# Gate rows by broadcast DMA, a transpose moved one step earlier, and three groups of instructions dealt later

## The chip, the cores and the metric

The kernel runs on one core of a Trainium2 chip. Its engines run side by side, each with its own instruction order: PE (TensorE, matrix products and transposes), DVE (VectorE), ACT (ScalarE), POOL (GpSimd), and SP, which here only issues DMA transfers. The metric is the device time of one execution in microseconds.

## What is computed

Two transformer-like blocks on x [1024, 1024] in fp32. The lines that matter:

```python
# first block
h = rms_norm(x, pre_mix_g) * (1.0 + sc1) + sh1         # sh1, sc1, g1, ...: silu(c) @ w_ada + b_ada
proj = h @ w_in                                        # qk_ml, v_ml, o_ml, gates, q_at, kv_at
h_ml = mlstm_chunkwise(q_ml, k_ml, v_ml, i_pre, logf)  # 4 heads of 128
h_ml = rms_norm(h_ml, ml_norm_g) * sigmoid(o_ml)
o_at = rms_norm(sliding_window_attention(q_at, k_at, v_at, attn_sinks), attn_norm_g)  # 8 heads of 64, window 128
x = x + g1 * rms_norm(concatenate([h_ml, o_at]) @ w_out, post_mix_g)
x = x + g2 * rms_norm(conv_ffn(rms_norm(x, pre_ffn_g) * (1.0 + sc2) + sh2), post_ffn_g)   # width 2816
# second block
x = x + concatenate([attention(h), pool_mixer(h)]) @ w_out_2          # h = rmsnorm(x, norm1_g_2) @ w_in_2
h = rmsnorm(x, norm2_g_2)
x = x + (silu(h @ w_gate_2) * (h @ w_up_2)) @ w_down_2                # width 2816
```

## The kernel before

The 1024 rows are eight tiles of 128 (`NT`). Every large fp32 product is made of three products of a split operand: `split` (lines 107 to 118) writes a high part (on ACT, POOL or DVE, lines 113 to 117) and, on DVE, the rest (line 118); `mm3` issues the three matmuls (lines 123 to 125). `sums_turn` transposes a tile of h (line 1313), scales it on ACT into `rawB` (lines 1297, 1299) and, for tiles 4 to 7, makes sums and differences of tiles on DVE (line 1317); `sums_split` and `part_of` split them. `one`, `two`, `three` and `five` are the products of an FFN that makes seven products of half-blocks instead of eight; `prep_first`, `prep_b1` and `prep_b2` load and split its weights. `sums_tile` is `sums_turn` and, for the first four tiles, `sums_split`.

SBUF tiles come from pools of few slots (U has 17, W 11, R 3), and PSUM from the banks that `psum(d, m, f)` sets out: in the first mixer two tiles D of two banks (`Dps`), two M (`Mps`) and two F (`Fps`); at an FFN's start two M and six F. A tile waits for the last reader of the slot that it takes. The order in which the functions are called is the program's order. A planner then deals the instructions to the engines: each engine runs its instructions in the dealt order, chosen by the planner's own costs and, among instructions that are ready by these costs, by program order. All DMAs go through SP's queue, in its order; a transfer that waits for data holds those behind it.

The stages that the change touches, in order of time:

- The opening, `start`: it loads the tiles of x (line 350), makes the shift `shp` in PSUM, copies it to SBUF as `sh` on ACT (line 362), and then normalises tile by tile (`norm`, lines 367 to 375), tile 0 with `shp` (line 372) and the others with `sh` (line 374); `to_hT` transposes (line 174).
- The sliding-window attention in `mixer1`: a loop over 16 jobs (tile n, head group g) with `turn`, `scores`, `q_stage` and, three steps behind (`LAG`), `values`. Behind a tile's second group, `values` squares the tile on ACT (line 527), sums the squares over the partitions by four products with a column of ones into an F bank (line 530, eight PE instructions as the trace counts them), copies the sum to `rat` (line 531), scales the tile on POOL (line 532) and stores it in `oad` (line 533). Behind the loop `rat` is turned into a factor, and a loop over eight groups of the q/k product (`m`) follows.
- `gates` leaves in `A` one row of 128 numbers for each of 32 pairs of chunk and head.
- The mLSTM loop at the end of `mixer1`: steps t = 0 to 10. A step does `ml_prep(t-3)` (transposes of a chunk's h, line 644, and its split `ho`, lines 647 and 648), `ml_front(t)`, `ml_mid(t-1)`, `at_part(t-2)`, for some t `tr(t-4)` (`sums_turn` of a finished tile), and `ml_part(t-3)` (the product of `ho` with its addition at line 659, post-norm, residual, store to `x1d` at line 663, pre-norm). `ml_front` loads `v` and `ogd` of a chunk into `vo` (lines 832, 833), spreads the gate rows of its four heads over the partitions by four products of 32 rows (line 836) into an M bank, adds, masks (line 838), exponentiates (839), multiplies by the k·q products (842, 843), and transposes k (850). `ml_mid` uses the result W a step later (line 882).
- The end of that loop and the start of the first FFN (lines 693 to 725).
- The second FFN's entry: a loop over tiles n (lines 1251 to 1268) that loads x3, adds the output product in two halves of 512 columns (line 1259), stores x4 (1262), normalises (POOL, 1265), and calls `sums_tile(n-1)` between the two halves; behind it `one(0)`, `sums_tile(7)`, `one(1)` to `one(3)`.

The loop of the second FFN's entry in short:

```python
for half in range(2):
    ...                                                   # 12 matmuls into ps
    nc.vector.tensor_tensor(xr[:, hs], xr[:, hs], ps, op=ALU.add)      # L1259
    if n and not half:
        self.sums_tile(h4.pop(n - 1), n - 1)
nc.sync.dma_start(out=self.x4d[n * P:(n + 1) * P, :], in_=xr)          # L1262
```

## Time and profile before

| | us |
|---|---|
| median of 3 executions (lowest to highest) | 2372.38 (2372.25 to 2374.23) |
| the profiled execution | 2373.33 |
| span of the profiled execution | 2371.5 |
| PE busy | 2275.5 (96%) |
| DVE busy | 1548.6 (65%) |
| ACT busy | 936.0 (39%) |
| POOL busy | 483.1 (20%) |
| mean granted clock of PE | 0.988 of full speed |

The page gives the busy time of each engine over the whole span. Its chain of work that ended last, followed back from the end, is almost all PE. The trace can then be asked for a stretch: busy time by engine, the waits of an engine by line with what released it ("PE f L123 <- ACT ho L647" is a wait of PE at line 123, for tile f, released by ACT's writing of `ho` at line 647), and the instructions in order of time. Times count from the span's start. The name of a tile (f, m and d are PSUM banks) stands before the line; PEld is PE's weight load, beside its matmuls.

### The profile page before, as it was taken

How to read it: one execution, taken by the hardware profiler on the slowest of the kernel's cores; microseconds unless marked ns; L12 is line 12 of the kernel's file. 1: busy time of each engine (PE TensorE's matmuls, PEld its weight loads, DVE VectorE, ACT ScalarE, POOL GpSimd, SP SyncE). 2: the span in 40 equal slices, each digit the busy share in tenths (PEclk: the TensorE clock that was granted, in tenths of full speed). 3: DMA queues.
4: the chain of work that ended last, by engine and by line, in shares of the span. 5: the costliest groups of instructions: out<-in, count | busy, mean ns of one | idle time of the engine just before them, and what ended most of it. 6: DMA issues, size and time to landing. Idle time of an engine off the chain costs nothing. (4 is left out here: it accounts for less than half of the span.)

```text
span 2371.5 us, 28426 instructions
## 1 busy us (share of the span) xinstructions
PE 2275.5 (96%) x10735; PEld 1855.0 (78%) x10735; DVE 1548.6 (65%) x2058; ACT 936.0 (39%) x1712; POOL 483.1 (20%) x570
## 2 busy tenths in 40 slices
PE   6999999998999999999989898999899999999999
PEld 3878888886787888888877786887678888888887
DVE  6757667568987777766566447995675555556661
ACT  3356424565544444511133227995542222231110
POOL 3146422232000100000021236763200000000000
PEclk9999999999999999999999999999999999999999
DMA  8612325421232222453122320001332222245301
GB/s 300 209 35 76 117 64 160 156 83 64 99 110 77 80 87 80 158 186 112 63 90 82 100 96 16 21 1 63 117 114 80 80 80 80 80 168 213 95 31 71
DMA packets 75619, 236.85 MB, mean 100 GB/s; under 512 B 11213, under 2 KB 16077, under 8 KB 75482
## 3 DMA queue, kind: packets, MB, share of 16 engines
q1 hardware_dynamic: 75482, 235.04, 29.4%
q8 instruction: 84, 1.38, 0.2%
q14 instruction: 53, 0.43, 0.1%
HBM read 184.66 MB, written 50.35 MB: 99 GB/s over the span
## 5 line engine op out<-in xcount | busy, mean ns | idle before, releaser
L123 PE MATMUL f<-h,sh 128*128 128x512 f32 x1232 | 482.8, 396 | 7.0 <-DVE d L1431 2.6
L124 PE MATMUL f<-h,sh 128*128 128x512 f32 x1232 | 485.4, 394 | 2.2 <-DVE h L118 2.2
L125 PE MATMUL f<-h,sl 128*128 128x512 f32 x1056 | 416.4, 395 | 0.1
L123 PEld LDWEIGHTS f<-h,sh 128*128 128x128 f32 x1232 | 232.0, 188 | 66.9 <-ACT d L1448 5.6
L1015 DVE TENSOR_TENSOR y<-y,f 128x512 f32<-128x512 f32 x240 | 161.2, 683 | 176.0 <-PE f L125 175.7
L124 PEld LDWEIGHTS f<-h,sh 128*128 128x128 f32 x1232 | 231.8, 188 | 55.9 <-DVE h L118 3.1
L125 PE MATMUL f<-h,h 128*128 128x512 f32 x704 | 274.1, 389 | 0.5 <-DVE h L118 0.5
L123 PE MATMUL f<-h,h 128*128 128x512 f32 x704 | 274.3, 390 | 0.0
L124 PE MATMUL f<-h,h 128*128 128x512 f32 x704 | 273.9, 389 | 0.0
L125 PEld LDWEIGHTS f<-h,sl 128*128 128x128 f32 x1056 | 198.6, 188 | 46.8 <-DVE sl L118 1.0
L117 POOL TENSOR_SCALAR sh<-raw 128x1024 fp32r<-128x1024 f32 x36 | 47.9, 1330 | 681.9 <-DVE sl L118 501.9
L125 PEld LDWEIGHTS f<-h,h 128*128 128x128 f32 x704 | 132.1, 188 | 28.3 <-DVE h L118 0.9
L124 PEld LDWEIGHTS f<-h,h 128*128 128x128 f32 x704 | 132.2, 188 | 27.5
L123 PEld LDWEIGHTS f<-h,h 128*128 128x128 f32 x704 | 132.2, 188 | 27.3
L123 PE MATMUL f<-hi,h 128*128 128x512 f32 (+2 forms) x384 | 141.0, 367 | 1.2 <-ACT qr L470 0.9
L125 PE MATMUL f<-hi,h 128*128 128x512 f32 (+2 forms) x384 | 138.2, 360 | 2.2 <-DVE h L178 2.2
L124 PE MATMUL f<-lo,h 128*128 128x512 f32 (+2 forms) x384 | 138.4, 360 | 0.0
L118 DVE TENSOR_TENSOR sl<-raw,sh 128x1024 fp32r<-128x1024 f32 x88 | 112.2, 1275 | 15.8 <-ACT sh L113 11.4
L117 POOL TENSOR_SCALAR h<-raw 128x1024 fp32r<-128x1024 f32 x26 | 32.2, 1239 | 411.0 <-PE f L125 164.4
L1452 DVE TENSOR_TENSOR d<-d,f 128x512 f32<-128x512 f32 x44 | 30.2, 686 | 118.9 <-PE f L125 118.9
L113 ACT ACTIVATE h<-raw 128x1024 fp32r<-128x1024 f32 x26 | 27.4, 1056 | 186.4 <-PE f L125 117.6
L113 ACT ACTIVATE sh<-raw 128x512 fp32r<-128x512 f32 (+1 forms) x96 | 80.1, 862 | 33.5 <-DVE raw L1403 30.5
(329 smaller groups left out, 4595.2 us busy)
## 6 DMA issues: line engine op xcount, KB each, us to landing
ada<-w_ada SPq DMA_DIRECT2D x48, 512.0 KB, 5.1
raw<-w_up SPq DMA_DIRECT2D x48, 512.0 KB, 4.2
raw<-w_gu SPq DMA_DIRECT2D x48, 512.0 KB, 3.8
raw<-w_down SPq DMA_DIRECT2D x44, 512.0 KB, 4.1
hr<-hidd SPq DMA_DIRECT2D x44, 512.0 KB, 5.5
hidd<-z SPq DMA_DIRECT2D x22, 512.0 KB, 2.6
hidd<-d SPq DMA_DIRECT2D x22, 512.0 KB, 2.7
raw<-w_out SPq DMA_DIRECT2D x16, 512.0 KB, 4.9
```

The source lines that it names most:

```text
L113: nc.scalar.activation(hi, src, AF.Copy)
L117: nc.gpsimd.tensor_scalar(hi, src, 1.0, 0.0, op0=ALU.mult, op1=ALU.add)
L118: (lo_eng or nc.vector).tensor_tensor(lo, src, hi.bitcast(F32), op=ALU.subtract)
L123: nc.tensor.matmul(out, a[0], b[0], start=start, stop=False, skip_group_check=more)
L124: nc.tensor.matmul(out, a[0], b[1], start=False, stop=False, skip_group_check=more)
L125: nc.tensor.matmul(out, a[1], b[0], start=False, stop=stop, skip_group_check=more)
L1015: nc.vector.tensor_tensor(y[:, hs], y[:, hs], ps, op=ALU.add)
L1452: nc.vector.tensor_tensor(d[:, 512:1024], d[:, 512:1024], c, op=ALU.add)
```

## The change

- In `start`, ACT's copy of `sh` comes between `norm(0)` and `norm(1)` instead of ahead of the loads of x.
- In `values`, the square stays; the sum of squares by PE, the copy to `rat`, POOL's product and the store go into `values_end`, which is called one step later ahead of the next `values`. The last one, and the factor `rat`, move into the q/k loop at m = 1.
- `gates` stores its 32 rows `A` to DRAM (`gated`), and `ml_front` loads a chunk's four rows, spread to 128 partitions (256 KB), into the upper half of `w1` by DMA, in place of the four products into an M bank.
- At the end of the mLSTM loop `ml_prep(7)` comes a step sooner, behind the new `psum`; `ml_part(6)` goes ahead of `sums_split(0)` and `tr(4)`; `tr(5)` and `sums_split(2)` go behind `ml_part(7)`.
- In the second FFN's entry `sums_tile(n-1)` follows both halves of tile n, and `one(1)` goes ahead of `sums_tile(7)`.

```diff
--- before.py
+++ after.py
@@ -309,6 +309,7 @@
         self.modr = self.dp.tile([6, D], F32, name="modr")
         self.vmd = self.dp.tile([NT, P, 512], F32, name="vmd")
         self.ogd = self.dp.tile([NT, P, 512], F32, name="ogd")
+        self.gated = self.dp.tile([32, P], F32, name="gated")
         self.oad = self.dp.tile([NT, P, 512], F32, name="oad")
         self.x1d = self.dp.tile([S, D], F32, name="x1d")
         self.x2d = self.dp.tile([S, D], F32, name="x2d")
@@ -358,8 +359,6 @@
         sh = self.U(name="sh")[:, 0:1024]
         self.w_load(2)
         for n in range(1, NT):
-            if n == 1:
-                nc.scalar.activation(sh, shp, AF.Copy)
             load_x(n)
             self.w_load(3)
         hT = self.new_hT()
@@ -376,6 +375,7 @@
 
         self.mods, self.mod_slot = self.mod_steps(), self.U
         norm(0)
+        nc.scalar.activation(sh, shp, AF.Copy)
         norm(1)
         wv = [self.w_next(0) for _ in range(4)]
         for n in range(NT):
@@ -525,6 +525,11 @@
             if g == 1:
                 sq = oT[n][:, 512:1024].rearrange("p (j t) -> p j t", j=4)
                 nc.scalar.activation(sq, o, AF.Square)
+
+        def values_end(t):
+            n, g = jobs[t]
+            if g == 1:
+                o, sq = (oT[n][:, i:i + 512].rearrange("p (j t) -> p j t", j=4) for i in (0, 512))
                 mp = self.Fps()
                 for j in range(4):
                     nc.tensor.matmul(mp[:, 0:1], sq[:, j], self.ones[:, 0:1], start=(j == 0), stop=(j == 3))
@@ -585,12 +590,13 @@
                     w0 = self.w_next(0)
                     d0 = self.Dps()
                 self.form_a(hT, w0, d0, (t - len(jobs),))
+            if t > LAG:
+                values_end(t - LAG - 1)
             if t >= LAG:
                 values(t - LAG)
         while og < 4:
             o_proj(og, wo)
             og += 1
-        rat = self.rstd(rat, 8, 1.0 / 512)
         gates = self.gate
 
 
@@ -600,6 +606,9 @@
         QK = {}
         for m in range(8):
             d = self.form_a(hT, self.w_next(1)) if m else d0
+            if m == 1:
+                values_end(len(jobs) - 1)
+                rat = self.rstd(rat, 8, 1.0 / 512)
             z = self.U(name="z")[:, 0:1024]
             nc.scalar.activation(z, d, AF.Identity, bias=wh[:, 32 + m:33 + m], scale=taps[:, m, 3:4])
             for j in range(1, 4):
@@ -668,7 +677,7 @@
             self.sums_turn(ys.pop(n), n)
 
         for t in range(NT + 3):
-            if t >= 3:
+            if 3 <= t < NT + 2:
                 ml_prep(t - 3)
             if t < NT:
                 state[t] = self.ml_front(t, gates, q_of, k_of)
@@ -693,19 +702,19 @@
                     self.ffn1_start()
                 if t == NT + 1:
                     self.psum(0, 2, 6)
+                    ml_prep(NT - 1)
                 if 4 <= t < NT:
                     tr(t - 4)
                 if t == NT:
                     self.prep_first(0)
+                ml_part(t - 3)
                 if t == NT + 1:
                     self.sums_split(0)
                     tr(4)
-                ml_part(t - 3)
-                if t == NT + 1:
                     self.sums_split(1)
-                    tr(5)
                     self.prep_first(1)
-                    self.sums_split(2)
+        tr(5)
+        self.sums_split(2)
         self.sums_split(3)
         tr(6)
         self.one(0)
@@ -821,6 +830,7 @@
         nc.scalar.activation(col[:, K:4 * K], col[:, K:4 * K], AF.Exp)
         cols = lambda i, c: col[:, i * K + 4 * c:i * K + 4 * c + 4]
         self.gate = A, cols
+        nc.sync.dma_start(out=self.gated, in_=A)
 
     def ml_front(self, c, gates, q_of, k_of):
         nc, C = self.nc, self.C
@@ -831,9 +841,8 @@
         nc.gpsimd.memset(v[:, :, 128:129], 1.0)
         nc.sync.dma_start(out=v[:, :, 0:128], in_=self.vmd[c].rearrange("p (h c) -> p h c", h=4))
         nc.sync.dma_start(out=vo[:, 516:1028], in_=self.ogd[c])
-        ab = self.Mps()
-        for h in range(4):
-            nc.tensor.matmul(ab[:, h * P:(h + 1) * P], self.ident[0:32, 4 * c + h:4 * c + h + 1].broadcast_to([32, P]), A, start=True, stop=True)
+        ab = w1[:, 512:1024]
+        nc.sync.dma_start(out=ab, in_=self.gated[4 * c:4 * c + 4, :].rearrange("h t -> (h t)").partition_broadcast(P))
         for h in range(4):
             nc.vector.scalar_tensor_tensor(W[:, h], ab[:, h * P:(h + 1) * P], col(0, c)[:, h:h + 1], C("mlmask"), op0=ALU.add, op1=ALU.min)
         nc.scalar.activation(W, W, AF.Exp)
@@ -1257,8 +1266,8 @@
                 for j in range(4):
                     self.mm3(ps, (ao[:, 0, j], ao[:, 1, j]), tuple(x[:, hs] for x in wa[j]), j == 0, j == 3)
                 nc.vector.tensor_tensor(xr[:, hs], xr[:, hs], ps, op=ALU.add)
-                if n and not half:
-                    self.sums_tile(h4.pop(n - 1), n - 1)
+            if n:
+                self.sums_tile(h4.pop(n - 1), n - 1)
             nc.sync.dma_start(out=self.x4d[n * P:(n + 1) * P, :], in_=xr)
             r = self.rstd(self.sumsq(xr), 1)
             t = h4[n] = self.U(name="h4")[:, 0:1024]
@@ -1267,8 +1276,9 @@
                 self.prep_first(n - 3, self.W if n == 6 else self.U)
         self.one(0)
         self.prep_b1(0, self.R)
+        self.one(1)
         self.sums_tile(h4.pop(7), 7)
-        for p in (1, 2, 3):
+        for p in (2, 3):
             self.one(p)
         self.sums_end()
         self.prep_b2(0)
```

## Rows read from the trace of the kernel before

**Rows 1.** Engine table of the page: busy us (share of the span) xinstructions.

```profile
PE 2275.5 (96%) x10735; PEld 1855.0 (78%) x10735; DVE 1548.6 (65%) x2058; ACT 936.0 (39%) x1712; POOL 483.1 (20%) x570
```

**Rows 2.** Stretches: from:to, us, busy PE PEld DVE ACT POOL, clock, DMA, GB/s.

```profile
372.00:505.00 133.00, 128.16 (x721) 108.38 (x721) 81.59 (x162) 72.35 (x180) 30.32 (x50) 0.99 0.42 141
416.00:424.00 8.00, 5.89 (x34) 5.72 (x35) 4.14 (x11) 4.08 (x10) 1.05 (x1) 0.79 1.02 384
454.62:473.32 18.70, 18.01 (x106) 15.19 (x106) 11.38 (x23) 11.50 (x31) 4.88 (x9) 1.00 0.28 87
...
244.00:252.00 8.00, 8.00 (x44) 7.60 (x45) 5.50 (x7) 4.78 (x17) 6.54 (x6) 0.57 0.54 158
...
1631.00:1720.00 89.00, 77.14 (x358) 60.72 (x357) 44.20 (x65) 42.77 (x107) 25.05 (x33) 1.00 0.33 115
...
1740.00:2360.00 620.00, 620.00 (x2703) 507.37 (x2702) 338.93 (x429) 142.68 (x173) 32.34 (x29) 1.00 0.29 100
```

**Rows 3.** Timeline of PE behind 540: start, us, line, operation, tile, [idle before].

```profile
540.80 0.67 PE L123 MATMUL f<-h,ho 128*128 128x512 f32 x1 [3.59 <-ACT ho L647]
...
544.26 0.45 PE L124 MATMUL f<-h,sh 128*128 128x512 f32 x1
```

**Rows 4.** Timeline of PE in the opening.

```profile
37.15 1.09 PE L174 MATMUL m<-cst,x 128*128 128x128 f32 x8 [2.37 <-DVE x L372]
...
44.53 1.06 PE L174 MATMUL m<-cst,x 128*128 128x128 f32 x8 [0.44 <-DVE x L374]
```

**Rows 5.** PE waits, 165 to 300: us in total, times, longest.

```profile
PE f L530 <- ACT oT L527: 6.5, 5, 3.4
```

**Rows 6.** Timeline of PE at one chunk's gates' rows.

```profile
372.38 1.15 PE L836 MATMUL m<-gateA,cst 32*128 32x128 f32 x8
373.46 0.94 PE L842 MATMUL m<-QK,QK 128*128 128x128 f32 x6
```

**Rows 7.** PE waits, 372 to 505.

```profile
PE m L842 <- DVE ho L648: 2.2, 1, 2.2
PE m L850 <- DVE w L838: 1.8, 3, 0.7
```

**Rows 8.** Transfers of tile vo, the chunk's loads.

```profile
DMA to landing us min/median/max: 2.7/3.5/6.9
```

**Rows 9.** Timeline of SP's queue in chunk 6.

```profile
471.15 0.53 SPq L832 DMA_DIRECT2D vo<-vmd  x1
477.96 0.33 SPq L663 DMA_DIRECT2D x1d<-xr  x1
```

**Rows 10.** Timeline of DVE in chunk 6.

```profile
473.32 0.60 DVE L838 SCALAR_TENSOR_TENSOR w<-m,col,cst 128x128 f32<-128x128 f32 x2
```

**Rows 11.** POOL's instructions of line 1265: min/median/max ns, first and last start.

```profile
L1265 POOL TENSOR_SCALAR h<-x,rstd x8: 1122/1122/2196, 1640.3 to 1708.9; 128x1024 f32<-128x1024 f32 x8
```

**Rows 12.** PE waits, 520 to 600.

```profile
PE f L123 <- ACT ho L647: 3.6, 1, 3.6
...
PE m L1313 <- POOL y L665: 1.7, 1, 1.7
PE m L644 <- ACT rawB L1299: 1.2, 1, 1.2
```

**Rows 13.** PE waits, 1630 to 1740.

```profile
PE m L1313 <- POOL h L1265: 8.4, 8, 2.0
PE f L123 <- DVE d L1431: 2.6, 1, 2.6
PE f L123 <- DVE x L1259: 0.9, 2, 0.6
```

**Rows 14.** Timeline of DVE in the second FFN's entry.

```profile
1644.07 0.69 DVE L118 TENSOR_TENSOR h<-rawB,h 128x512 fp32r<-128x512 f32 x1 [5.95 <-POOL h L117]
1644.67 0.68 DVE L1259 TENSOR_TENSOR x<-x,f 128x512 f32<-128x512 f32 x1
...
1652.56 0.69 DVE L118 TENSOR_TENSOR h<-rawB,h 128x512 fp32r<-128x512 f32 x1 [6.01 <-POOL h L117]
```

## What the change does to the time: the prediction

> **What bounds the kernel now.** I read the page's engine table first: PE is busy 2275.5 us of a span of 2371.5 [rows 1], so all PE idle time together is 96 us, and an edit can pay in three ways only: by taking instructions off PE, by removing some of that idle time, or by keeping PE at the full clock. Then the table by stretches [rows 2]. From 1740 to 2360 PE is busy 620.00 of 620 us: nothing there can be won without fewer instructions, and the change has no line there, so that stretch moves earlier or later as a block. It also gives the price of one matmul: 620.00 / 2703 = 0.23 us. The stretches with holes are the ones the change edits: 4.8 us idle in 372 to 505 (the mLSTM loop), 11.9 in 1631 to 1720 (the second FFN's entry). Two short stretches show a second cost of a hole: PE's granted clock is 0.57 in 244 to 252, right behind a wait, against 1.00 where PE is fed. And behind the wait that ends at 540.80 eight matmuls take until 544.26, 3.46 / 8 = 0.43 us each instead of 0.23 [rows 3]: the lower of the two levels, 1.2 GHz. The PE waits of each stretch, grouped by line, say which edit meets which hole.
>
> The profiled execution took 2373.33 us, 1.8 over its span and 0.95 over the median of 2372.38. I make the sum against 2373.33 and take off 1 us for the median.
>
> **Part A, the copy of sh in the opening.** ACT's L362 moves behind the first tile's normalisation. PE waits 2.37 us for the first tile [rows 4], of which DVE's wait for that copy is a part, so tile 0 can come 1 us sooner (the copy's own length). I count 0: the second tile's transposes are late as well, waiting 0.44 us on its own addition [rows 4], and they hang on x loads that are not moved. Whatever tile 0 gains, PE waits for tile 1 instead. Bounds -1 (ACT's copy now stands ahead of tile 0's eviction on ACT and would delay it by 1 us) to +1.
>
> **Part B, the square sums a step later.** PE waits 6.5 us in five places for the square (L530 behind ACT's L527), the longest 3.4 us by the trace's list [rows 5]. The eight PE instructions, the copy, POOL's product and the store to `oad` all run later; `oad` is read only in the mLSTM loop, so the store has no reader near, but the last one, `rat`, and POOL's product now share their engines with the first q/k product. Two things keep the gain small. The planner deals the order of each engine, so a PE instruction that waits may stand ahead of others that could not start either, and then the wait only changes its name. And `mp` keeps one of only two F banks into the next step, right ahead of the `ov` product that wants one. I take +1, nearest to the short waits among the five; the upper bound is +5 (6.5 less what other waits then take, with clock: 8 us at 0.57 is 8 x 0.43 = 3.4 us of lost work in 244 to 252), the lower -2 (one more F-bank wait of the size of the shorter ones).
>
> **Part C, gates' rows by DMA.** Eight times, PE does four fp32 products for the gates' rows: the group starts at 372.38 and the next matmul goes at 373.46 [rows 6], 1.08 us, and 8 x 1.08 = 8.6 us. In this loop PE is busy 18.01 of a step of 18.70 [rows 2], so this time is on the path. It also frees an M bank (of two) eight times: the 2.2 us wait of L842 for DVE's L648 is an M-bank wait, since L842 reads nothing of L648's, and the 1.8 us of L850 for L838 in three places is the same bank (L838 reads it) [rows 7]; the clock behind the first is 0.79 in 416 to 424, 8 x 0.21 = 1.7 us [rows 2]. What is added: one store of 16 KB, and eight loads of 256 KB on SP's queue, each about 0.4 us to issue. No trace of before has this load. The nearest is that of `vo` in the same step, issued by the same queue: 2.7 to 6.9 us to landing, median 3.5 [rows 8]. L838 has no wait on PE worth naming and its result is used by PE most of a step later, so a load that goes beside `vo` (471.15) and lands 3.5 us later makes L838 some 1.3 us later than its 473.32 [rows 8 to 10]; DVE is busy 11.38 of 18.70 [rows 2] and absorbs that. Upper bound 8.6 + 2.2 + 1.8 + 1.7 = 14.3. Lower bound 3, if the load lands at 6.9 and PE waits 0.7, the longest of L850's, in each of eight chunks (5.6 us). I take +8.6, the PE time alone: the waits may return in another form.
>
> In L838 the source changes from a PSUM bank to SBUF, beside a mask in SBUF. POOL's L1265, normally 1.122 us, once takes 2.196 with DVE at work [rows 11]; POOL is busy 4.88 us of a step [rows 2]. The Trainium skill ("SBUF — State Buffer", section "Who interferes with whom") says that a DVE instruction with two SBUF inputs contends with a POOL instruction that reads SBUF, and that the one which comes second is held for the whole of the other. The 2.196 agrees in kind. By that rule one block of 1.1 us a chunk would put up to 9 us on DVE and would turn C into nothing if PE waited for all of it; this is one way into rival 1.
>
> **Part D, the end of the mixer.** `ml_prep(7)` moves from the last step into the one before, so its four transposes stand ahead of `ml_part(6)`. Today they wait 1.2 us for a bank from ACT (L1299), then the product waits 3.6 us for ACT's copy `ho` [rows 12], then eight matmuls run at the slow clock, 8 x (0.43 - 0.23) = 1.6 us [rows 3]. Sum 6.4. The last chunk's h comes out of `ml_mid(7)`, a step earlier, so the transposes can be early. `tr(5)` and `sums_split(2)` go behind the last product; they take their DVE and ACT work with them. I count +5: one of the neighbours will be late next, namely the transposes of the last tile and the splits that the first FFN products read. Bounds 0 (DVE is what is late: the splits now come after) to +8 (6.4 and the 1.7 us that the transposes L1313 wait for POOL in that stretch [rows 12]).
>
> **Part E, the second FFN's entry.** Between 1631 and 1720 PE idles 11.9 us; 8.4 of it is eight waits of the transposes L1313 for POOL's h, 2.6 one wait at the end for DVE's d (L1431), 0.9 for L1259 [rows 13]. DVE's order shows a loop: for each tile L118 (split of tile n-1), L1259 (first half of tile n), L118, L1259; the L118 of 1644.07 returns at 1652.56, a period of 8.49 us [rows 14], while a tile has 24 matmuls x 0.23 = 5.5 us beside its eight transposes. The loop runs store, square sum, rstd, h, transposes, evictions, split, and only then the next tile's addition, which is queued behind the split on DVE. With the transposes behind both halves, the two L1259 come first in program order, so the next tile's chain starts one loop earlier, and POOL's h has 24 matmuls of cover instead of 12. At the end `one(1)` covers tile 7's chain. Nothing is removed, so the upper bound is all idle, 12. The lower is 3: the store of tile n still stands ahead of the load of tile n+1 on SP, and the splits are as many. I take +8: most of 8.4 goes, as it is this wait that the move addresses; the 2.6 stays, for it is DVE's.
>
> Sum: 0 + 1 + 8.6 + 5 + 8 = 22.6. 2373.3 - 22.6 = 2350.7, some 2350 for the median.
>
> **Rivals.** *1. The waits move.* Off PE's path, DVE sets these stages, and each bank or engine that is freed is awaited one instruction later. For it: the change adds no engine time anywhere but removes PE time alone. Then C gives 8.6 - 3.8 (L850's 1.8 grows to 8 x 0.7 = 5.6) = 4.8, D 1.6 (clock only), E 4 (half), B 0: 10.4, or 2362. *2. Everything lands.* A 1, B 5, C 14, D 8, E 12: 40, or 2332. Against it: all of 40 would be nearly half of PE's idle and slow time in the kernel. *3. Slower, by the head of SP's queue.* SP issues in order, and the store of x1 (L663, 477.96) waits for DVE before it goes [rows 9]. If the load of a chunk's gate rows is dealt behind that store because its slot of the U pool comes free late, it goes at 478.3 and lands 3.5 later, 481.8: L838 is 8.5 us late against 473.32 [rows 10], and all of DVE's work queued behind it, the split `ho` of L648 included, which PE awaits. In the five steps with a store that is 5 x 8.5 = 42 us, less the 8.6 of C and the 14 of the other parts: about 2393. It decides from (8.6 + 14) / 5 = 4.5 us of lateness a step. Against it: `vo`, which takes a slot of the same pool in the same step, goes at 471.15 [rows 9]. *4. The planner deals as before*, or exchanges M-bank waits for F-bank waits, so that B, D and E do nothing and C's 8.6 is lost to the reordered steps: 2372.
>
> **How the numbers follow.** Chances: forecast (2342 to 2357) 0.58, rival 1 (2357 to 2367) 0.20, rival 2 (2330 to 2342) 0.10, rival 3 0.07, rival 4 0.05. The range leaves out rival 3, rival 4 and the ends of rivals 1 and 2 (some 0.04 each): 2336 to 2364. A difference of 0.2% (4.7 us) is about what a measurement of this kernel tells from none. Faster holds forecast, rivals 1 and 2: 0.88, less 0.01 for the end of rival 1; same 0.06; slower 0.07.
>
> **What would show it.** C: L836 gone, the step of the mLSTM loop 17.6 us instead of 18.7, the new load going beside `vo`, L838 with less than 1 us of DMA wait; a wait of L838 on the DMA over 4.5 us is rival 3. D: no wait of L123 for `ho` near 540 and a clock of 1.00 there. E: DVE's order L1259, L1259, L118, L118, the L1313 waits under 1 us in all, a period near 6.5. B: the L530 waits gone, with or without new waits at L470 or `ov`. A: tile 0 sooner, the wait for tile 1 longer by as much. I am wrong if 372 to 505 does not shrink by 8 us, or if the stretch behind 1740 is no longer gap-free, as all of the sum rests on that block sliding forward.

## The result and the profile after

The changed kernel takes 2360.53 us in the median of five executions (2354.38 to 2364.10); the kernel before takes 2372.38 (2370.51 to 2375.36). The ratio is 0.9942, with a 95% interval of 0.9932 to 0.9953. The medians make the change worth 11.9 us; the ratio, which is worked out from all executions, makes it 0.58% or 13.8 us. The forecast was 2350, with a range of 2336 to 2364; the time lies in the range's upper end, and some 9 to 11 of the 22.6 us that were forecast are missing.

The profiled execution of the changed kernel took 2364.10 us and is the longest of the five, so the two traces differ by only 9.2 us (2373.33 - 2364.10). To see where, I matched the DVE and ACT instructions of both traces by source line, tiles and order, and took the median difference of their starts within 10 us of a point of the kernel before. Negative is earlier. The same was done for the traces of the experiments below.

| offset in us at | 115 | 165 | 300 | 360 | 520 | 590 | 1600 | 1740 |
|---|---|---|---|---|---|---|---|---|
| changed kernel | +2.5 | +4.5 | +8.6 | +8.8 | -1.3 | -3.0 | -2.6 | -9.6 |
| without A (e1) | +0.7 | +3.3 | +6.1 | +6.1 | -3.1 | -5.1 | -5.1 | -14.4 |
| without B (e2) | +4.3 | +4.3 | +2.6 | +2.5 | -4.3 | -6.6 | -8.6 | -19.7 |
| C, D and E (e3) | -0.4 | -0.3 | -1.9 | -1.5 | -9.8 | -11.6 | -11.7 | -21.7 |
| A alone (e4) | +2.7 | +3.1 | +2.8 | +2.9 | +2.4 | +2.9 | +3.4 | +2.5 |
| B alone (e5) | -0.2 | 0.0 | +4.9 | +5.2 | +1.8 | +2.8 | +0.7 | -0.2 |
| C alone (e6) | +0.2 | +0.4 | -1.1 | -1.1 | -9.4 | -8.1 | -8.5 | -8.5 |
| D alone (e7) | +0.6 | +0.8 | +0.7 | +0.9 | -2.5 | -3.2 | -1.8 | -2.9 |
| E alone (e8) | 0.0 | 0.0 | 0.0 | +0.1 | -2.7 | -1.0 | 0.0 | -10.7 |
| C, D, E, no square sums (e9) | -1.7 | -1.5 | -4.1 | -5.6 | -13.3 | -17.4 | -17.6 | -28.5 |
| C, D, E, shift from PSUM (e10) | -0.3 | +0.7 | +2.2 | +2.3 | -7.6 | -9.4 | -9.9 | -19.4 |
| C, D, E, product first (e11) | 0.0 | +0.1 | -1.2 | -0.8 | -9.3 | -9.0 | -9.6 | -19.6 |
| C, D, E, no load (e12) | -0.2 | +0.8 | +0.9 | +0.9 | -10.0 | -11.8 | -10.6 | -21.6 |

In the changed kernel the work up to 165 loses 4.5 us (2.5 of them before 115), the attention another 4.1; the mLSTM loop (360 to 520) gains 10.1, its end 1.7, the second FFN's entry 7.0. Behind that entry PE is busy 621.00 of 621 us (1729 to 2350), so that this block slid forward whole, as the sum assumed. Of the 10.1 up to 3 belong to the execution of before that was profiled: B, D and E alone, whose mLSTM loop up to 505 is that of the kernel before, come out of it 3.4, 3.4 and 2.8 us earlier than it did (A alone 0.5), with shorter M-bank waits in it. Of one or two us in this table, then, a part can be the execution.

The engine table answers [rows 1]: PE has 64 instructions fewer in the record and 6.6 us less busy time, 64 being what the trace counts for the gates' products.

```profile
PE 2268.9 (96%) x10671; PEld 1851.3 (78%) x10671; DVE 1553.0 (66%) x2058; ACT 934.0 (40%) x1712; POOL 483.7 (20%) x570
```

In the opening, PE waits 1.3 us for tile 0 and 3.9 for tile 1, where [rows 4] had 2.4 and 0.4. Two of PE's waits between 28 and 70:

```profile
PE m L174 <- DVE x L373: 3.9, 1, 3.9
...
PE m L174 <- DVE x L371: 1.3, 1, 1.3
```

In the attention the long square-sum wait of [rows 5] is still there, at line 535, and the other waits there have become waits for M banks (lines 815, 765 and 792 behind DVE's line 508) and, at line 486, for ACT. All waits of PE there sum to 11.5 us, where the kernel before had 9.1. PE's longest between 165 and 305:

```profile
PE m L815 <- DVE pt L508: 3.3, 1, 3.3
PE f L535 <- ACT oT L527: 3.2, 1, 3.2
PE m L765 <- DVE pt L508: 1.8, 4, 0.8
PE d L486 <- ACT p L492: 1.8, 2, 1.1
PE m L792 <- DVE pt L508: 0.8, 1, 0.8
```

In the mLSTM loop, L836 is gone. Where [rows 7] had 2.2 us at L842 and 1.8 at L850, the k transposes (now line 859) wait 4.3 us once, for the same DVE instruction (`ho`, now line 657), and 0.5:

```profile
PE m L859 <- DVE ho L657: 4.3, 1, 4.3
PE m L859 <- DVE w L852: 0.5, 1, 0.5
```

At the end of the loop the 3.6 us for `ho` of [rows 12] are gone, and tile 5's transposes wait 3.5 us for POOL's pre-norm. Two of PE's waits between 520 and 592:

```profile
PE m L1323 <- POOL y L674: 3.5, 1, 3.5
...
PE m L1323 <- ACT rawB L1309: 0.7, 1, 0.7
```

The slow clock has moved with the wait. It stood behind the wait for `ho` before, and stands behind the wait for POOL now (columns as in [rows 2]; the kernel before, then the changed one):

```profile
540.00:544.00 4.00, 3.20 (x8) 2.55 (x9) 3.29 (x5) 0.75 (x2) 0.84 (x2) 0.62 0.00 0
```

```profile
548.00:552.00 4.00, 4.00 (x15) 3.29 (x14) 3.22 (x4) 2.03 (x6) 0.70 (x2) 0.58 0.00 0
```

In the second FFN's entry DVE's order is the one that I expected, two additions (now line 1268) and then the splits, and the period has gone from the 8.49 us of [rows 14] to 6.4 us in the first tiles. PE sets it now: it has no idle time from 1635 to 1664, and its transposes start 6.41 and 6.42 us apart. DVE's additions wait 0.7 and 0.4 us for the load of x3, but PE does not wait for them. PE's timeline and then DVE's:

```profile
1640.14 1.03 PE L1323 MATMUL m<-cst,h 128*128 128x128 f32 x8
...
1646.55 1.04 PE L1323 MATMUL m<-cst,h 128*128 128x128 f32 x8
...
1652.97 1.03 PE L1323 MATMUL m<-cst,h 128*128 128x128 f32 x8
```

```profile
1640.13 1.28 DVE L1268 TENSOR_TENSOR x<-x,f 128x512 f32<-128x512 f32 x2 [4.64 <-DMA x<-x3d]
1642.65 0.69 DVE L118 TENSOR_TENSOR h<-rawB,h 128x512 fp32r<-128x512 f32 x1 [1.24 <-POOL h L117]
...
1645.95 1.49 DVE L1268 TENSOR_TENSOR x<-x,f 128x512 f32<-128x512 f32 x2 [0.72 <-DMA x<-x3d]
...
1652.08 0.69 DVE L1268 TENSOR_TENSOR x<-x,f 128x512 f32<-128x512 f32 x1 [0.38 <-DMA x<-x3d]
```

From tile 4 on, where DVE makes the sums of tiles as well, the additions are 9.4 to 10.2 us apart (1660.10, 1670.31, 1679.76, 1689.15), and what PE still waits for POOL falls there. It is to be held against the 8.4 us of [rows 13]; the 2.6 us at L1431 and the 0.9 at L1259 are gone:

```profile
PE m L1323 <- POOL h L1274: 4.8, 3, 2.8
```

### The profile page after: what moved, and what is told of

It is laid out like the page before. It is cut to its first block, busy times and chain, and to the rows that moved or that the text cites. A ratio compares the mean times of both kernels' runs of the same rounds, so it can differ in the third digit from the quotient of the medians.

```text
span 2362.3 us, 28309 instructions
## 1 busy us (share of the span) xinstructions
PE 2268.9 (96%) x10671; PEld 1851.3 (78%) x10671; DVE 1553.0 (66%) x2058; ACT 934.0 (40%) x1712; POOL 483.7 (20%) x570
## 5 line engine op out<-in xcount | busy, mean ns | idle before, releaser
L125 PEld LDWEIGHTS f<-h,h 128*128 128x128 f32 x704 | 132.2, 188 | 28.5 <-DVE h L118 0.9
L118 DVE TENSOR_TENSOR sl<-raw,sh 128x1024 fp32r<-128x1024 f32 x88 | 113.4, 1289 | 11.1 <-ACT sh L113 10.6
```

The lines of the kernel that those rows point to most:

```text
L118: (lo_eng or nc.vector).tensor_tensor(lo, src, hi.bitcast(F32), op=ALU.subtract)
L125: nc.tensor.matmul(out, a[1], b[0], start=False, stop=stop, skip_group_check=more)
```

## Experiments

Each was timed beside the kernel before on the same chip; that one's medians were 2372.2 to 2373.6. A time alone is a median, with the lowest and highest behind it, and the interval behind a ratio to the kernel before is its 95% interval. Each cut of a diff says against which kernel it is; "..." marks lines left out.

**The changed kernel without part A (e1).**

Against the changed kernel:

```diff
+            if n == 1:
+                nc.scalar.activation(sh, shp, AF.Copy)
             load_x(n)
...
-        nc.scalar.activation(sh, shp, AF.Copy)
```

> The changed kernel with part A (the copy of sh in the opening) undone. Theory 1, A costs time: in the trace of the changed kernel the second tile's transposes wait 3.9 us for DVE's addition of sh, 0.4 before, and the work behind is 2.5 us late from 60 to 115 and 4.4 us late from 120 on. Without A these go: 2360.5 - 4.4 = 2356, and the wait at the second tile is again near 0.4. Theory 2, this lateness is the loads of x in that one execution (the five executions of the changed kernel spread over 10 us), and not the edit: the time stays at 2360 within 2 us.

Measured: 2358.7 (2352.4 to 2360.5), ratio 0.9939 (0.9927 to 0.9951). That is 1.8 us under the changed kernel by the medians and 0.7 by the ratios, between the two theories and not to be told from either by itself. The trace takes theory 1's side for the opening: tile 1's wait is 0.4 us again and the offset is +0.7 from 70 to 115 instead of +2.5; a lateness of 2.6 between 115 and 135 comes in its place.

**The changed kernel without part B (e2).**

Against the changed kernel; the lines of `values_end` fall back into `values`:

```diff
-        def values_end(t):
...
-            if t > LAG:
-                values_end(t - LAG - 1)
...
+        rat = self.rstd(rat, 8, 1.0 / 512)
...
-            if m == 1:
-                values_end(len(jobs) - 1)
-                rat = self.rstd(rat, 8, 1.0 / 512)
```

> The changed kernel with part B (the square sums a step later) undone. Theory 1, B costs what the trace shows between 165 and 290, where the changed kernel falls back from 4.5 us late to 8.6 us late: 4.1 us, so 2356. Theory 2, B gives its forecast 1 us and the fall-back is a consequence of the late opening (loads that come at another point of the loop): then undoing it gives 2361.

Measured: 2356.4 (2354.5 to 2360.7), ratio 0.9940 (0.9928 to 0.9952). The median is 4.1 us under the changed kernel's, as theory 1 has it, but the ratios differ by only 0.5 us, so the times do not decide. The trace takes theory 1's side: the attention gains 1.7 us (+4.3 to +2.6) where it lost 4.1. That gain itself is the execution's, for e3 and e6, whose engines run the attention in the order of the kernel before, gain 1.6 and 1.5 there.

**C, D and E alone (e3).** Both of the edits above together, against the changed kernel:

```diff
+            if n == 1:
+                nc.scalar.activation(sh, shp, AF.Copy)
...
-            if t > LAG:
-                values_end(t - LAG - 1)
```

> Parts A and B both undone, C, D and E kept. Theory 1, both cost what the trace shows, 8.6 us together: 2352, near my forecast of 2350, and the work behind 290 stands where it stood before. Theory 2, the parts behind gain less when the front is not late (the mLSTM loop of the changed kernel gains 9.8 us from a late start, which may be loads that had more time): then 2356 to 2360.

Measured: 2352.3 (2348.8 to 2353.4), ratio 0.9916 (0.9903 to 0.9929): 8.2 us under the changed kernel by the medians, 6.2 by the ratios, and 20.0 under the kernel before. Theory 1 holds. C, D and E were forecast at 8.6 + 5 + 8 = 21.6. Of the kernels that compute everything this is the fastest.

**A alone (e4).** Against the kernel before:

```diff
-            if n == 1:
-                nc.scalar.activation(sh, shp, AF.Copy)
...
         norm(0)
+        nc.scalar.activation(sh, shp, AF.Copy)
         norm(1)
```

> The kernel before with part A alone. Theory 1: A costs 4.4 us, 2376.8. My prediction: A is worth 0, with bounds -1 to +1, 2371 to 2373. If neither holds and the time is lower, A helps through the order that the planner deals behind it.

Measured: 2374.4 (2373.5 to 2377.4), ratio 1.0009 (1.0000 to 1.0017): slower by some 2 us, at the edge of what the interval tells from nothing. In its trace the opening costs 3.1 us and nothing happens behind. The step that failed in my working can be read from the changed kernel's DVE, ACT and SP, first DVE in the opening:

```profile
37.65 1.27 DVE L369 SCALAR_TENSOR_TENSOR x<-x,rstd,bv 128x1024 f32<-128x1024 f32 x1
...
41.17 1.28 DVE L369 SCALAR_TENSOR_TENSOR x<-x,rstd,bv 128x1024 f32<-128x1024 f32 x1
42.88 1.29 DVE L369 SCALAR_TENSOR_TENSOR x<-x,rstd,bv 128x1024 f32<-128x1024 f32 x1 [0.43 <-POOL rstd L159]
44.88 1.28 DVE L369 SCALAR_TENSOR_TENSOR x<-x,rstd,bv 128x1024 f32<-128x1024 f32 x1 [0.71 <-POOL rstd L159]
46.08 3.49 DVE L373 TENSOR_TENSOR x<-x,sh 128x1024 f32<-128x1024 f32 x3
```

then ACT's copy of `sh`:

```profile
41.11 1.01 ACT L378 ACTIVATE sh<-d 128x1024 f32<-128x1024 f32 x1
```

and SP's queue, in the changed kernel and in the kernel before:

```profile
25.84 6.73 SPq L351 DMA_DIRECT2D x<-x  x6
```

```profile
33.88 3.56 SPq L350 DMA_DIRECT2D x<-x  x7
```

I had taken the x loads as unmoved. Without a copy ahead of them they are dealt 8 us sooner (one at 23.28 and six from 25.84; in the kernel before seven from 33.88). Tile 1 can be scaled at 37.65, 4.2 us sooner than before. But its addition of `sh` (line 373) waits until 46.08. First the copy is missing: ACT makes it at 41.11, behind the square sums of three later tiles. Then the planner's order on DVE holds the addition, with the scalings of tiles 2 to 4 ahead of it, of which two wait for POOL's factors of the later tiles. In the kernel before that addition started at 43.16.

**B alone (e5).** Against the kernel before:

```diff
+        def values_end(t):
...
+            if t > LAG:
+                values_end(t - LAG - 1)
...
-        rat = self.rstd(rat, 8, 1.0 / 512)
...
+            if m == 1:
+                values_end(len(jobs) - 1)
+                rat = self.rstd(rat, 8, 1.0 / 512)
```

> The kernel before with part B alone. My prediction: a gain of 1 us, 2371 (bounds 2367 to 2374). What the runs so far say: with A in place B costs 1.8 us (2358.7 with B and without A against 2352.3 without both is 6.4 us; 2360.5 against 2356.4 is 4.1), so 2376 to 2379.

Measured: 2376.2 (2370.8 to 2379.5), ratio 1.0013 (1.0004 to 1.0022): slower by 3 to 4 us (0.9 to 5.2 by the interval), the other way than I forecast. PE's waits in the attention, to be held against the 6.5 us in five of [rows 5]:

```profile
PE m L765 <- DVE pt L508: 3.7, 4, 2.3
PE f L535 <- ACT oT L527: 3.2, 1, 3.2
PE d L486 <- ACT p L492: 1.9, 3, 1.1
PE m L815 <- DVE pt L508: 1.8, 1, 1.8
```

The short waits at the square sum are gone, the longest stays (3.2 of 3.4), and 3.7 + 1.8 us of M-bank waits behind DVE's line 508 appear, where the kernel before had 0.9 + 0.8. All of PE's waits there sum to 11.9 us against 9.1. The clock around them falls as well (columns as in [rows 2]):

```profile
220.00:240.00 20.00, 16.67 (x80) 13.54 (x80) 14.76 (x30) 11.72 (x34) 8.20 (x11) 0.84 0.27 91
240.00:260.00 20.00, 16.77 (x91) 15.60 (x90) 12.83 (x19) 8.48 (x25) 9.32 (x8) 0.73 0.34 106
```

The kernel before has a clock of 1.00 from 220 to 240 and 0.83 from 240 to 260. At 228 B alone is some 2.5 us earlier than the kernel before, at 260 5.4 later. Of the 2.5 only about 1 can be B's: PE's clock from 175 to 185 is 0.83 in the kernel before, but 1.00 in B alone and in e3, and e3, which runs the old order there, is 1.5 us earlier behind that stretch as well. The loss of nearly 8 falls in the stretch where DVE also splits `w_out` weights and does the gates' scans.

**C alone (e6).** Against the kernel before; the new tile `gated` is left out:

```diff
+        nc.sync.dma_start(out=self.gated, in_=A)
...
-        ab = self.Mps()
-        for h in range(4):
-            nc.tensor.matmul(ab[:, h * P:(h + 1) * P], self.ident[0:32, 4 * c + h:4 * c + h + 1].broadcast_to([32, P]), A, start=True, stop=True)
+        ab = w1[:, 512:1024]
+        nc.sync.dma_start(out=ab, in_=self.gated[4 * c:4 * c + 4, :].rearrange("h t -> (h t)").partition_broadcast(P))
```

> The kernel before with part C alone. My prediction: a gain of 8.6 us, 2363.7, the matmuls' own time. Rival 1 (the waits come back at L850 and elsewhere): 4.8, 2367.5. If the M bank's waits and the clock behind them go too: 2358.

Measured: 2366.4 (2365.0 to 2369.6), ratio 0.9978 (0.9969 to 0.9988): 5.8 us by the medians, 2.8 to 7.4 by the interval. Less than 8.6, and nearer to rival 1's 4.8. In its trace the loop gains 8.3 us (360 to 520), with this wait left in it between 360 and 510:

```profile
PE m L851 <- DVE ho L649: 4.9, 2, 4.6
```

**D alone (e7).** Against the kernel before:

```diff
-            if t >= 3:
+            if 3 <= t < NT + 2:
                 ml_prep(t - 3)
...
                     self.psum(0, 2, 6)
+                    ml_prep(NT - 1)
...
+                ml_part(t - 3)
                 if t == NT + 1:
...
-                ml_part(t - 3)
-                if t == NT + 1:
                     self.sums_split(1)
-                    tr(5)
                     self.prep_first(1)
-                    self.sums_split(2)
+        tr(5)
+        self.sums_split(2)
```

> The kernel before with part D alone. My prediction: a gain of 5 us, 2367.3. Rival 1 (the wait moves to the neighbours, only the clock behind it is won): 1.6, 2370.7. The trace of the changed kernel shows 1.8 between 520 and 590.

Measured: 2370.5 (2364.7 to 2375.4), ratio 0.9994 (0.9984 to 1.0003). Within 0.2% of no change, and the size that rival 1 has: 1.7 us by the medians (between 0.7 lost and 3.8 gained by the interval).

**E alone (e8).** Against the kernel before:

```diff
-                if n and not half:
-                    self.sums_tile(h4.pop(n - 1), n - 1)
+            if n:
+                self.sums_tile(h4.pop(n - 1), n - 1)
...
+        self.one(1)
         self.sums_tile(h4.pop(7), 7)
-        for p in (1, 2, 3):
+        for p in (2, 3):
```

> The kernel before with part E alone. My prediction: a gain of 8 us, 2364.3. Rival 1 (half of the wait moves): 4 us, 2368.3. The trace of the changed kernel shows 7.1 between 1620 and 1740, so 2365.2.

Measured: 2366.2 (2361.7 to 2369.1), ratio 0.9968 (0.9956 to 0.9981): 6.1 us by the medians, 7.6 by the ratio. The forecast of 8 lies in the interval (4.5 to 10.4). Its trace gains 10.7 from 1600 to 1740, and PE still waits for POOL there, 2.3 of the 8.4 us before:

```profile
PE m L1314 <- POOL h L1265: 2.3, 3, 1.9
```

**C, D and E without the square sums (e9).** The attention's output is left without its norm. Against C, D and E (e3), as in the three that follow:

```diff
+        nc.gpsimd.memset(rat, 512.0)
...
-                mp = self.Fps()
-                for j in range(4):
-                    nc.tensor.matmul(mp[:, 0:1], sq[:, j], self.ones[:, 0:1], start=(j == 0), stop=(j == 3))
-                nc.scalar.copy(rat[:, n:n + 1], mp[:, 0:1])
```

> Parts C, D and E on the kernel before, with the attention's square sums left out of the computation (the 64 PE instructions of line 530 and the copies to rat; rat is a constant, so the attention's output is not normalised). The square sums' own PE time is some 0.95 us for each of 8 tiles, 7.6 us. Theory 1, the 6.5 us of waits at line 530 only name a lateness that DVE and the banks bring about anyway: the time falls by no more than 7.6 from 2352.3, to 2345 or above, and M-bank waits on DVE's line 508 take the place of those waits. Theory 2, the waits belong to the square sums, so a better place for them is worth having: it falls by 7.6 + 6.5 or more, to 2338.

Measured: 2348.2 (2344.5 to 2349.4), ratio 0.9898 (0.9883 to 0.9913), 4.1 us under C, D and E. Theory 2's 14 us are out, and theory 1 holds: taking the products away altogether, with their 7.6 us of PE time and their 6.5 us of waits, is worth less than the PE time by the medians. The longest waits that take their place between 160 and 300:

```profile
PE m L754 <- DVE pt L510: 3.3, 4, 2.1
PE f L123 <- DVE oT L766: 2.8, 1, 2.8
PE d L488 <- ACT p L494: 2.6, 2, 2.2
PE f L521 <- ACT pt L509: 1.0, 1, 1.0
```

These four make 9.7 us of waits behind DVE and ACT; with the smaller ones it is 12.6, where the kernel before had 9.1 with the square sums' 6.5 among them. So it is unlikely that any other place for them would have won the 6.5.

**C, D and E with tiles 0 and 1 shifted from PSUM (e10).**

```diff
-            if n == 1:
-                nc.scalar.activation(sh, shp, AF.Copy)
...
-            if not n:
+            if n < 2:
                 nc.vector.tensor_tensor(xs[n], xs[n], shp, op=ALU.add)
...
         norm(1)
+        nc.scalar.activation(sh, shp, AF.Copy)
```

> Parts C, D and E, and another form of A: tiles 0 and 1 both take the shift from PSUM, and the copy to sh comes behind them. Theory 1, A cost time because tile 1 then waited for a copy that stands on ACT behind the square sums of later tiles and, on DVE, because its addition stood behind the scalings of tiles that were not loaded: with no copy ahead of tile 1 the first tile comes 1.1 us sooner as in A and the second does not wait, so 1 to 3 us faster than C, D and E, 2349.5 to 2351.3. Theory 2, the loads of x set the second tile whatever stands there: 2352 or, as with A, 2354.4.

Measured: 2354.9 (2353.3 to 2356.7), ratio 0.9924 (0.9912 to 0.9937). Theory 1's cause is right, and its gain did not come. DVE now adds the shift to tile 1 at 39.96, behind its scaling and tile 0's evictions, and its transposes wait for nothing; the offset at 115 is -0.3, where A alone has +2.7. But C, D and E have -0.4 there: what tile 0 gains goes into a wait of 1.8 us for DVE's split of a weight (line 118). The attention behind it loses 1.5 us (+0.7 at 165, +2.2 at 300), where e3 gains 1.6, although PE, DVE, ACT and POOL run it in the same order and PE's waits are the same. What differs is the clock: 1.00 in e3 from 175 to 185 and 0.83 from 240 to 260, where this trace has 0.83 and 0.74. No run shows why. DVE in the opening:

```profile
37.57 1.27 DVE L369 SCALAR_TENSOR_TENSOR x<-x,rstd,bv 128x1024 f32<-128x1024 f32 x1
38.76 1.28 DVE L178 TENSOR_TENSOR h<-m,h 128x512 fp32r<-128x512 f32 x2
39.96 1.20 DVE L371 TENSOR_TENSOR x<-x,d 128x1024 f32<-128x1024 f32 x1
```

**C, D and E with the first FFN's product ahead of tile 5's transposes (e11).**

```diff
-        tr(5)
         self.sums_split(2)
         self.sums_split(3)
+        self.one(0)
+        tr(5)
         tr(6)
-        self.one(0)
```

> Parts C, D and E, and behind the last mixer product the first FFN's first product, one(0), ahead of the transposes of tiles 5 and 6. In C, D and E the transposes of tile 5 wait 3.5 us for POOL's pre-norm, as the mixer's product waited 3.6 for ho in the kernel before. Theory 1, that chain is only a latency and 5.5 us of matmuls cover it: 3 us less, 2349.3. Theory 2 (rival 1 for part D), DVE sets this stage and PE waits somewhere else: 2352 within 1 us.

Measured: 2354.1 (2351.8 to 2355.2), ratio 0.9920 (0.9906 to 0.9933), 1.8 us over C, D and E: theory 2. The 3.5 us for POOL are gone, and a wait of 6.3 us for ACT's eviction of another tile stands in their place, between 500 and 592:

```profile
PE m L1315 <- ACT rawB L1301: 6.3, 1, 6.3
```

**C, D and E without the load of the gates' rows (e12).**

```diff
-        ab = w1[:, 512:1024]
-        nc.sync.dma_start(out=ab, in_=self.gated[4 * c:4 * c + 4, :].rearrange("h t -> (h t)").partition_broadcast(P))
         for h in range(4):
-            nc.vector.scalar_tensor_tensor(W[:, h], ab[:, h * P:(h + 1) * P], col(0, c)[:, h:h + 1], C("mlmask"), op0=ALU.add, op1=ALU.min)
+            nc.vector.scalar_tensor_tensor(W[:, h], self.ones, col(0, c)[:, h:h + 1], C("mlmask"), op0=ALU.add, op1=ALU.min)
```

> Parts C, D and E with the load of the gates' rows left out: line 838 adds a constant tile of ones in SBUF instead of the rows, so the mLSTM's weights lack them. It prices the load by itself. The trace of C, D and E shows DVE waiting 4.6 us in four places for that load, which takes 4.5 to 7.2 us to land. Theory 1, DVE has idle time in each step and absorbs it, as I predicted: 2352.3 within 1 us. Theory 2, DVE's waits reach PE: up to 4.6 us faster, 2347.7, and the M-bank wait of line 850 for ho (4.2 us) shrinks.

Measured: 2351.4 (2348.8 to 2352.7), ratio 0.9905 (0.9892 to 0.9919), 0.9 us under C, D and E by the medians and 2.6 by the ratios, whose intervals overlap. The times lean to theory 1 and the waits take its side. In the trace of C, D and E, DVE waits for the load at line 839 four times, and the load's landing is in the answer for line 837:

```profile
  DMA w<-gated: 4.6, 4
```

```profile
DMA to landing us min/median/max: 4.5/5.9/7.2
```

Little of these 4.6 us reaches PE. Its waits between 360 and 512 sum to 5.6 us with the load and 4.3 without it, and the M-bank wait for `ho` stays at 4.3:

```profile
PE m L849 <- DVE ho L649: 4.3, 1, 4.3
```

## Why the prediction was half right

The time lies in the range because the range is wide: the losses of A and B were outside their own bounds. C, D and E together came to 20.0 of the 21.6 us.

**A: wrong.** Forecast 0, measured 2.1 us lost alone (none to 4.0 by the interval). At 115 the three traces with A in this form are 2.5 to 4.3 us late and the others 1.7 us early to 0.7 late. The step that failed is "x loads that are not moved": the copy stood ahead of them, so moving it moves them, and DVE's order with them. The 1 us that tile 0 was to gain was there (2.4 to 1.3 us of waiting), and the loss at tile 1 was three times as large, as [rows 4] had no row for a DVE order that did not exist yet. My bound of -1 left out a re-dealt order. e10 shows the cause in the opening by taking the copy from tile 1's path. That the changed kernel is another 2 us late between 115 and 135 is not settled: it does so without A too (e1), but not with B alone (e5) nor with A, C, D and E (e2), so B and one of C, D and E are in it together.

**B: wrong, and outside its bounds.** Forecast a gain of 1 with -2 to +5, measured 3 to 4 us lost. From 165 to 300 the three traces with B lose 2.8 to 4.9 us; the nine others that have the square sums lie between 1.7 gained and 1.5 lost, all with one order of PE, DVE, ACT and POOL. The step that failed is the bound of "one more F-bank wait": I wrote that the wait may only change its name; e5 shows that it did, into M-bank waits behind line 508, with 2.8 us more of waits in all and a lower clock, and e9 that even without the products no more than their own time is won. Missing was a price for the re-dealt order where DVE has most to do. That it is DVE's order which does it (its score maximum, line 489, comes behind two weight splits at 230.3 and 232.9, the first of which waits 2.7 us for POOL) I read from the trace and did not try by itself.

**C: right in mechanism, too high by about a third.** 8.6 forecast, 5.8 alone. The load costs little (0.9 us by the medians of e12) though it lands in 5.9, far from the 3.5 that I took from `vo` [rows 8], and DVE absorbs most of it, as forecast. Rival 3's queue did not come about either: the load is issued beside `vo`, and DVE's waits for it sum to 3.6 us in the whole loop in the changed kernel and 4.6 in e3, over my sign of less than 1, but far from the 4.5 a step at which that rival decides. Line 838, with both sources in SBUF, stays at its 0.34 us in the median, with single long instructions. The kernel before, the changed kernel and e11:

```profile
L838 DVE SCALAR_TENSOR_TENSOR w<-m,col,cst x32: 321/343/352, 377.9 to 495.7; 128x128 f32<-128x128 f32 x32
```

```profile
L847 DVE SCALAR_TENSOR_TENSOR w<-w,col,cst x32: 339/344/630, 391.3 to 496.6; 128x128 f32<-128x128 f32 x32
```

```profile
L839 DVE SCALAR_TENSOR_TENSOR w<-w,col,cst x32: 336/346/1196, 381.4 to 488.7; 128x128 f32<-128x128 f32 x32
```

In eight of the nine traces with C two or three of these 32 instructions take 0.48 to 1.20 us (e12 has none). Each of them overlaps a POOL instruction of 1.0 to 1.6 us and ends 0.1 to 0.2 us behind it. The Trainium skill's rule on a DVE instruction with two SBUF inputs ("SBUF — State Buffer", section "Who interferes with whom") says that it contends with a POOL instruction that reads SBUF. These rows agree with it, and they price it: 0.5 to 1.9 us of DVE time in a trace, against the 9 that I had as the most. (The 2.196 of [rows 11], which I gave as happening once, is the longest of three: three of those eight instructions take 2.16 to 2.20, each beside a DVE instruction of line 118.)

What is missing is one wait. In the five traces with the loop of the kernel before PE waits 0.4 to 2.2 us for the first chunk's `ho` (2.2 in [rows 7]); in all nine with C, the one without the load among them, 3.7 to 4.6 us at a time. The split `ho` is DVE's and got no earlier (counted from each loop's start, 424.10 - 8.8 in the changed kernel and 416.30 - 0.9 in D alone), so what PE saves in the chunks ahead of that point is waited away there. The products of four chunks lie ahead of it (that of the fourth just before), up to 4 x 1.08 = 4.3 us. Behind that point C gives more than I forecast. PE's step, from one chunk's transposes (line 644) to the next, is 18.4 to 18.8 us in three steps and 17.3 to 17.4 in the next in the kernel before and in A, B, D and E alone; it is 16.5 to 17.2 and 16.0 to 16.2 in the changed kernel, e3, e6 and e12, where I expected 17.6. Beside the 1.08 us, the waits of L850 for L838 [rows 7], 0.6 us in each of three, are gone there. That is some 7 us in four steps, while the step with the wait for `ho` grew, from between 17.5 and 20.9 to between 21.7 and 23.1. That account is worked out from the traces and was not tried by itself.

**D: the size was off, and rival 1 named the reason.** Forecast 5, measured 1.7 alone and 1.7 in the changed kernel's trace. The 3.6 us for `ho` went as planned; "one of the neighbours will be late next" took 3.5 of it, tile 5's transposes for POOL, and the slow clock came behind that wait (0.58 from 548 to 552) as it had behind the other. So the 1.6 us of clock, on which rival 1's size rests, were not won either, and that its number came out is luck. What fell is PE's idle time between 500 and 592, from 10.8 to 9.0 us. e11 moved the wait for POOL too, and the next, for ACT, was longer. In these two orders a wait for another engine took the place of the one that was removed; which engine sets this stage was not tried further.

**E: right in size, in part for another reason.** Forecast 8, measured 6.1 to 7.6 alone and 7.0 in the changed kernel's trace. The DVE order and the period (6.4, forecast near 6.5) are as forecast in the first tiles. "Most of 8.4 goes" is not: the L1313 wait shrank to 4.8 in the changed kernel, where I had put it under 1, and to 2.3 alone. The rest of the gain is the 2.6 at L1431, which I had left in place, and the 0.9 at L1259. That these made up the difference is luck.

Of the whole: C, D and E were forecast at 21.6 and gave 20.0 together (16.8 to 23.0 by the interval), though alone they add up to only 13.6. The uncertainties of the three, some 2 to 3 us each, nearly cover the difference, and the table of offsets closes most of it. As an estimate, take the mean gain of the traces that have a part in its stretch, less that of those that don't, the kernel before among them with 0: C 8.9 - 2.0 = 6.9 (360 to 520), D 1.7 + 0.9 = 2.6 (520 to 590, without e9 and e11), E 9.9 - 0.6 = 9.3 (1600 to 1740). That makes 18.8, so nothing asks for the three to help each other. A and B were forecast at +1 and cost 8.2 together by the medians (6.2 by the ratios). The time fell into the interval of rival 1 (2357 to 2367), but not by rival 1: it wanted E halved and B at nothing, and the loss came from two edits that were counted as harmless.

## What to carry to other kernels

Where a planner deals the order, an edit that removes no instruction has no "nothing" as its lower bound: price it by the largest wait of the stretch that it re-deals, and look for the loads that it lets go earlier. Moving the instruction that a wait names helped where DVE was half idle (E, busy 44.2 of 89.0 us before), and mostly renamed the wait where DVE had more to do (B, 97.7 of 140.0, and D, 68.1 of 92.0); three stages are no proof that its load decides. Work taken off the engine that sets the pace paid from the point on where no other engine set it, even though the replacement is slow to arrive (C).

## What the runs showed of the hardware

The 256 KB load that spreads four rows of 512 bytes over 128 partitions takes 4.5 to 7.2 us to land in e3, 5.9 in the median, against 2.7 to 6.8 and 3.5 for the `vo` loads beside it, of 256 KB each. A DVE instruction of 0.34 us took up to 1.20 beside a POOL instruction once both its sources were in SBUF, and at most 0.35 in the kernel before, with one source in PSUM. And executions of one program differ by more than the kernel before led me to expect: 2354.4 to 2364.1 for the changed kernel. Part of it can be placed: the same M-bank wait in the unchanged mLSTM loop is 2.2 us in one trace and 0.4 in another (e7). PE's clock differs too where the order of the engines is the same: from 175 to 185 it is 0.83 in the kernel before and 1.00 in e3, which is 1.5 us earlier behind that stretch.
